# RG-LRU stage: TensorE's order written out, sigmoid work between the gates, PSUM banks of its own; the later adaLN vectors summed in the q/k/v stage

## The chip, the cores and the metric

The kernel runs on one core of a Trainium2 chip. The metric is the device time of one execution in microseconds (us). PE is TensorE, DVE is VectorE, ACT is ScalarE, POOL is GpSimd, and SP is SyncE, which here only issues DMAs. PSUM is the memory in which matmuls leave their results; it has eight banks per partition, each of 512 float32.

## What is computed

One backbone layer over 1024 latent tokens and 256 context tokens of width 1024, all in float32. Reduced to what matters here:

```python
mod = split(silu(c) @ w_ada + b_ada, 6)            # adaLN: shift/scale 1, gate 1, shift/scale 2, gate 2
z   = split(modulate(rmsnorm(x), mod[0], mod[1]) @ w_in, ...)   # rnn in, rnn gate, q, kv, k rope, merge gates
xr  = conv4(z[0])                                   # width-4 depthwise conv over the tokens
for d in (forward, backward):                       # RG-LRU, two directions
    r, i = sigmoid(xr @ wa[d] + ba[d]), sigmoid(xr @ wx[d] + bx[d])     # block diagonal, 8 blocks of 128
    a = exp(-8 * r * softplus(-lam[d]))
    h[d] = scan(a, sqrt(1 - a * a) * i * xr)
rnn = (h[0] + h[1]) * gelu(z[1])
q, k, v = latent attention projections of z[2:5], rms norms, rope
merged = sigmoid(z[5][0]) * (rnn @ w_rnn_out) + sigmoid(z[5][1]) * (attend(q, k, v) @ w_mla_out)
x = x + mod[2] * (merged @ w_o)
x = x + mod[5] * expert_choice_moe(modulate(rmsnorm(x), mod[3], mod[4]))
```

The vectors `mod[2]` to `mod[5]` (the "later" ones) are not needed before the RG-LRU branch is finished.

## The kernel before

Every float32 matmul is done as three matmuls on a high and a low part (`mm3`, lines 97 to 99: high by high, low by high, high by low). `split` (lines 93 and 94) makes the parts: ACT copies the high part (`wh`, `zh`), DVE subtracts it from the source (`wl`, `zl`). Weights come through a ring of four raw buffers called `wr`, which `nextw` keeps two items ahead.

The program runs through stages. In the first the tokens are normed and kept transposed in SBUF (`xh`, `xl`). In the **q/k/v stage** (function `qkv`, about 80 to 268 us) eight latent token tiles of 128 and then two context tiles are worked on one after the other. For a tile PE does three transposes (`tp`), the projection of the next tile (`zq`, 24 matmuls), `kv` (6), `qp` (12), and then as filling a block of 48 matmuls of the rnn gate or of a merge gate (`z1`, shown as `z`). DVE norms and ropes: `zn` is the normed projection, `kf` and `qf` are the keys and queries, and the rope is lines 439 to 444. The reciprocal roots are powers on POOL (line 142, tile `st`, widths 3, 8 and 16). `k_d`, `v_d`, `q_d`, `ge_d`, `s_d` are stores to DRAM. The Tile scheduler orders the instructions of each engine here.

In the **RG-LRU stage** (268 to 591.5 us) eight channel blocks are worked on. `conv_part` projects a block (`z0` for the latent tokens, shown as `z`, and `z0c` for the context), ACT evicts it (line 589) and DVE adds the other three conv taps (line 592). `lru_part` does the four gates: `gz` (6 matmuls) for the latent and `gc` (3) for the context tokens, each followed by sigmoids on ACT (lines 610 and 611). After tanh, exp and sqrt on ACT and the scans on DVE, `rn_d` is stored. `sig_block` is a merge gate: 48 matmuls into `zg`, a sigmoid and a store; `sig_plan` says how many follow each block (1, 1, 1, 2, 1, 1, 2, 3). ACT's order is written out by hand in this stage; PE's is the scheduler's.

The later adaLN vectors are summed here as well: `mod_step` loads 128 rows of `w_ada` (512 KB) and DVE multiplies them by `silu(c)` and adds them to `acc` (line 395); after eight steps two matmuls of ones with `acc` (`mp`, line 401) sum the partitions, ACT copies the row (line 402) into a tile of tag `sg`, and the row is stored to `mod_d`. Four steps are done after each `sig_block`, 32 in all. `MP2` and `N2` are the numbers of steps after each tile of the q/k/v stage and of all those done there: 1 and 0.

All PSUM tiles of both stages and of the next come from two rings: `a` with three tiles of two banks (`kv`, `qp`, `z1`, `z0`, `gz`, `zg`, `mp`, `ro`) and `b` with two of one bank (`tp`, `zq`, `z0c`, `gc`, `mc`, `lb`). After the RG-LRU stage `mc` and `lb` prepare the router, and `ro` (the rnn branch's output projection, with `rh` and `rl` read back from `rn_d`) begins.

Of the kernel before, what the change touches and what calls it, by code (L numbers as in the profile page):

```python
# [27 lines left out]
P = 128  # L28
# [32 lines left out]
def layer_kernel(ctx: ExitStack, tc: tile.TileContext, I, rope_tab, out, dbg=None):  # L61
# [268 lines left out]
    def nextw(shape):  # L330
        n = taken[0]
        assert items[n][1] == shape, (items[n], shape)
        taken[0] = n + LOOK
        fetch()
        taken[0] = n + 1
        return ahead[n]

    LOOK = 2
    NFIRST = 3
    MP2, N2 = 1, 0  # L340
# [45 lines left out]
    def mod_step(j):  # L386
# [9 lines left out]
        if k == KD - 1:  # L396
            row = mpool().tile([1, D], F32, name="g", tag="sg", bufs=1)
            mp = pa("mp")
            for n in range(2):
                sl = slice(n * 512, (n + 1) * 512)  # L400
                nc.tensor.matmul(mp[0:1, sl], ones, acc[:, sl], start=True, stop=True)
            nc.scalar.copy(row, mp[0:1, :])
            nc.sync.dma_start(mod_d[m:m + 1, :], row)
# [162 lines left out]

    p3c = pool("p3")
    p3 = p3c.__enter__()
    if True:
        p4c = None  # L570

        def sig_block(dst, mid=None):
            zz = pa("zg")
            zblock(zz)
            if mid:
                mid()
            if p4c:
                sg = wst.tile([P, SEQ], F32, name="wr", tag="wr", bufs=4)
            else:
                sg = p3.tile([P, SEQ], F32, name="sg", tag="sg", bufs=1)  # L580
            nc.scalar.activation(sg, zz, AF.Sigmoid)
            nc.sync.dma_start(dst, sg)

        def conv_part(b):
            zc, zz = pb("z0c"), pa("z0")
# [12 lines left out]
        def lru_part(b, xr, xrh, xrl):  # L598
            gh, gl_ = nextw([2, 2, P])
            gates = []  # L600
            for d in range(2):
                for g, bn in ((0, "ba"), (1, "bx")):
                    gc, gz = pb("gc"), pa("gz")
# [4 lines left out]
                    r = p3.tile([P, TOK], F32, name=("r", "i")[g], bufs=2)  # L608
# [4 lines left out]
            av, vv = [], []  # L613
            for d in range(2):
                v = p3.tile([P, TOK], F32, name="vv", bufs=2)
                nc.scalar.activation(v, gates[2 * d], AF.Tanh, scale=p8[:, d * 8 + b:d * 8 + b + 1])
                vv.append(v)
            for d in range(2):
# [28 lines left out]
            return rest  # L647
# [13 lines left out]
        with tc.manual_schedule(engines={mybir.EngineType.Activation}):  # L661
# [21 lines left out]
            for b in range(KD):  # L683
# [3 lines left out]
                rest = lru_part(b, *cur)  # L687
                if b + 1 < KD:
                    split(nxt[1], nxt[2], nxt[0])
                for n in range(sig_plan[b]):  # L690
                    w, bb = jobs.pop(0)
                    if b == KD - 1 and n == 1:
                        assert not steps
# [3 lines left out]
                    sig_block((s0_d, s1_d)[w][bb], rest if n == 0 else load_rn if b == KD - 1 else None)  # L697
                    for _ in range(4):
                        if steps:
                            mod_step(steps.pop(0))  # L700
            load_rn(KD)


    xnp.__exit__(None, None, None)
# [504 lines left out]
```

## Time and profile before

| | us |
|---|---|
| median of 3 runs | 1798.1 (1798.03 to 1804.27) |
| the profiled execution, its own time | 1810.5 |
| its span, first to last instruction | 1808.7 |
| mean granted TensorE clock | 0.972 |
| PE busy | 1693.9 (94%) |
| DVE, ACT, POOL busy | 1365.1, 1042.9, 272.9 |

The profile is of one execution, which took 12.4 us longer than the median of the runs; 1.8 us of its own time lie outside the span. A busy share is one of the whole span. An engine that idles costs nothing by itself: what matters is where PE, the busiest one, stands still, and what it waits for there.

### The profile page before, as it was taken

How to read it: one execution, taken by the hardware profiler on the slowest of the kernel's cores; microseconds unless marked ns; L12 is line 12 of the kernel's file. 1: busy time of each engine (PE TensorE's matmuls, PEld its weight loads, DVE VectorE, ACT ScalarE, POOL GpSimd, SP SyncE). 2: the span in 40 equal slices, each digit the busy share in tenths (PEclk: the TensorE clock that was granted, in tenths of full speed). 3: DMA queues.
4: the chain of work that ended last, by engine and by line, in shares of the span. 5: the costliest groups of instructions: out<-in, count | busy, mean ns of one | idle time of the engine just before them, and what ended most of it. 6: DMA issues, size and time to landing. Idle time of an engine off the chain costs nothing.

```text
span 1808.7 us, 21761 instructions
## 1 busy us (share of the span) xinstructions
PE 1693.9 (94%) x7769; PEld 1351.6 (75%) x7769; DVE 1365.1 (75%) x1840; ACT 1042.9 (58%) x1323; POOL 272.9 (15%) x204
## 2 busy tenths in 40 slices
PE   8999999999999999999999989809999999999996
PEld 4888888777778877777776767707888888888875
DVE  5754546997897445787885866587999999999996
ACT  3532325665676314677667443306777777777784
POOL 2033321121211100011110031310010011001000
PEclk8999999999999999999999998959999999999999
DMA  9255343455443943001000566468999999999971
GB/s 345 94 161 120 92 119 94 141 162 163 140 134 113 311 148 130 28 28 47 9 1 1 221 232 235 168 249 286 377 369 393 395 386 368 399 385 378 380 265 24
DMA packets 178380, 365.91 MB, mean 202 GB/s; under 512 B 43328, under 2 KB 93912, under 8 KB 178272
## 3 DMA queue, kind: packets, MB, share of 16 engines
q1 hardware_dynamic: 173664, 347.74, 53.4%
q0 software_dynamic: 4608, 16.78, 4.0%
q8 instruction: 61, 1.00, 0.2%
q14 instruction: 47, 0.39, 0.1%
HBM read 316.94 MB, written 47.54 MB: 202 GB/s over the span
## 4 chain that ended last, share of the span: by engine, by line
PE 67%; DVE 16%; issue 6%; ACT 5%; DMA 3%; POOL 2%; SPq 0%; POOLq 0%; DVEq 0%; ACTq 0%
PE w_e_gate L98 3%; PE w_e_up L98 3%; PE w_e_gate L97 3%; PE w_e_gate L99 3%; PE w_e_down L98 3%; PE w_e_up L99 3%; PE w_e_up L97 3%; PE w_e_down L99 3%; PE w_e_down L97 3%; PE pm L782 2%; POOL st L142 2%; PE s L97 2%; PE ro L97 2%; PE ro L99 2%; PE ro L98 2%
## 5 line engine op out<-in xcount | busy, mean ns | idle before, releaser
L94 DVE TENSOR_TENSOR wl<-ma,wh 128x1024 fp32r<-128x1024 f32 x198 | 236.1, 1220 | 21.5 <-ACT wh L93 14.8
L93 ACT CAST wh<-ma 128x1024 fp32r<-128x1024 f32 x198 | 206.7, 1053 | 57.0 <-PE w_e_down L99 18.1
L94 DVE TENSOR_TENSOR wl<-me,wh 128x1024 fp32r<-128x1024 f32 x142 | 170.0, 1220 | 20.4 <-ACT wh L93 14.4
L93 ACT CAST wh<-wr 128x1024 fp32r<-128x1024 f32 (+1 forms) x97 | 98.3, 1014 | 147.6 <-PE z L98 54.6
L93 ACT CAST wh<-me 128x1024 fp32r<-128x1024 f32 x142 | 148.3, 1053 | 45.7 <-PE w_e_down L99 15.6
L846 ACT ACTIVATE pr<-s 128x512 f32<-128x512 f32 x160 | 95.6, 599 | 75.4 <-PE s L99 74.0
L784 DVE TENSOR_REDUCE mx<-pm 128x1 f32<-128x320 f32 x256 | 114.5, 483 | 24.9 <-PE pm L782 22.6
L94 DVE TENSOR_TENSOR wl<-wr,wh 128x1024 fp32r<-128x1024 f32 (+1 forms) x97 | 114.5, 1188 | 22.5 <-ACT wh L93 20.7
L98 PE MATMUL z<-xl,wh 128*128 128x512 f32 x320 | 126.5, 396 | 0.8 <-DVE xl L279 0.8
L99 PE MATMUL z<-xh,wl 128*128 128x512 f32 x320 | 126.2, 395 | 0.6 <-POOL wl L325 0.6
L97 PE MATMUL z<-xh,wh 128*128 128x512 f32 x320 | 126.4, 397 | 0.0
L1155 POOL DMA_INDIRECT out_dram<-y,icol x16 | 36.3, 2266 | 494.5 <-DVE y L1154 494.5
L94 DVE TENSOR_TENSOR pl<-pr,ph 128x1024 fp32r<-128x1024 f32 x64 | 81.2, 1269 | 31.8 <-ACT ph L93 25.0
L98 PE MATMUL w_e_up<-wl,xgh 128*128 128x512 f32 x256 | 103.1, 403 | 1.0 <-DVE wl L94 0.9
L98 PE MATMUL w_e_gate<-wl,xgh 128*128 128x512 f32 x256 | 102.7, 401 | 0.0
L97 PE MATMUL w_e_gate<-wh,xgh 128*128 128x512 f32 x256 | 102.4, 400 | 0.0
L98 PE MATMUL w_e_down<-wl,hdh 128*128 128x512 f32 x256 | 101.6, 397 | 0.6 <-DVE wl L94 0.2
L99 PE MATMUL w_e_down<-wh,hdl 128*128 128x512 f32 x256 | 99.8, 390 | 0.8 <-DVE hdl L94 0.8
L99 PE MATMUL w_e_gate<-wh,xgl 128*128 128x512 f32 x256 | 100.3, 392 | 0.0
L97 PE MATMUL w_e_down<-wh,hdh 128*128 128x512 f32 x256 | 99.9, 390 | 0.2 <-ACT hdh L93 0.2
L97 PE MATMUL w_e_up<-wh,xgh 128*128 128x512 f32 x256 | 100.1, 391 | 0.0
L99 PE MATMUL w_e_up<-wh,xgl 128*128 128x512 f32 x256 | 100.1, 391 | 0.0
(336 smaller groups left out, 4433.3 us busy)
## 6 DMA issues: line engine op xcount, KB each, us to landing
ma<-in_w_e_down_dram SPq DMA_DIRECT2D x68, 512.0 KB, 8.5
ma<-in_w_e_gate_dram SPq DMA_DIRECT2D x66, 512.0 KB, 7.5
ma<-in_w_e_up_dram SPq DMA_DIRECT2D x64, 512.0 KB, 6.6
me<-in_w_e_gate_dram SPq DMA_DIRECT2D x48, 512.0 KB, 5.6
me<-in_w_e_up_dram SPq DMA_DIRECT2D x48, 512.0 KB, 7.0
me<-in_w_e_down_dram SPq DMA_DIRECT2D x46, 512.0 KB, 8.2
wr<-in_w_in_dram SPq DMA_DIRECT2D x32, 512.0 KB, 4.9
wr<-in_w_ada_dram SPq DMA_DIRECT2D x32, 512.0 KB, 3.5
```

What stands on the lines that cost most here:

```text
L93: nc.scalar.copy(h, src)
L94: nc.vector.tensor_tensor(l, src, h.bitcast(F32), OP.subtract)
L97: nc.tensor.matmul(o, lh, rh, start=start, stop=False)
L98: nc.tensor.matmul(o, lh, rl, start=False, stop=False)
L99: nc.tensor.matmul(o, ll, rh, start=False, stop=stop)
L142: nc.gpsimd.tensor_tensor(ap, ap, h, OP.pow)
L782: nc.tensor.matmul(pm[:, 0:320], qh[:, t * P:(t + 1) * P], kh[:, g * 320:(g + 1) * 320], start=True, stop=True)
L784: nc.vector.tensor_reduce(mx[:, g, t:t + 1], pm[:, 0:320], axis=AX.X, op=OP.max)
L846: nc.scalar.activation(pr[:, sl], sp_, AF.Exp)
L1155: nc.gpsimd.indirect_dma_start(out=out_rows, out_offset=bass.IndirectOffsetOnAxis(ap=icol[:, e:e + 1], axis=0), in_=y, in_offset=None, com ...
```

## The change

1. `MP2, N2 = 4, 4 * KD`: all 32 `mod_step`s are done in the q/k/v stage, four after each of its first eight tiles. Their loads, sums, `mp` matmuls and stores move there. The row is copied into `acc` itself and stored from there.
2. In the RG-LRU stage PE's order is written out too. `sig_mm` is a generator that gives the 48 matmuls of a sigmoid block in eight pieces of six; one piece follows each gate, the other four pieces follow the gates. For that a weight is taken earlier (`look`, `look_ahead`).
3. The stage has its own PSUM pool `ps3`: `z0c` one bank, `gc` one bank, `gz` one buffer of two banks, and `z` (for `z0` and `zg`) a ring of two. After the stage another pool `ps4` has the rings `a` and `b` again.
4. A direction's tanh follows its two gates, and `r` has three buffers.

```diff
@@ -327,17 +327,23 @@
                 split(h, l, raw)
             ahead.append((h, l))
 
-    def nextw(shape):
+    def nextw(shape, look=None):
         n = taken[0]
         assert items[n][1] == shape, (items[n], shape)
-        taken[0] = n + LOOK
+        taken[0] = n + (LOOK if look is None else look)
         fetch()
         taken[0] = n + 1
         return ahead[n]
 
+    def look_ahead():
+        n = taken[0]
+        taken[0] = n - 1 + LOOK
+        fetch()
+        taken[0] = n
+
     LOOK = 2
     NFIRST = 3
-    MP2, N2 = 1, 0
+    MP2, N2 = 4, 4 * KD
 
     def zhalf(dst, h, l, n, ks=range(KD)):
         sl = slice(CTX + n * 512, CTX + (n + 1) * 512)
@@ -394,7 +400,7 @@
         nc.sync.dma_start(raw, w_ada[k * P:(k + 1) * P, (2 + m) * D:(3 + m) * D])
         nc.vector.scalar_tensor_tensor(acc, raw, sc[:, k, 0:1], acc, op0=OP.mult, op1=OP.add)
         if k == KD - 1:
-            row = mpool().tile([1, D], F32, name="g", tag="sg", bufs=1)
+            row = acc[0:1, :]
             mp = pa("mp")
             for n in range(2):
                 sl = slice(n * 512, (n + 1) * 512)
@@ -564,14 +570,31 @@
                     mod_step(steps.pop(0))
 
 
+
+
+    assert not steps
+    open_psum("ps3")
+
+    def pz(name):
+        return ps["p"].tile([P, 1024], F32, name=name, tag="z", bufs=2)
+
     p3c = pool("p3")
     p3 = p3c.__enter__()
     if True:
         p4c = None
 
-        def sig_block(dst, mid=None):
-            zz = pa("zg")
-            zblock(zz)
+        def sig_mm(look=None):
+
+            zz = pz("zg")
+            h, l = nextw([KD, P], look)
+            for n in range(2):
+                for k in range(0, KD, 2):
+                    zhalf(zz, h, l, n, (k, k + 1))
+                    yield zz
+
+        def sig_block(dst, mid=None, mm=None):
+            for zz in mm or sig_mm():
+                pass
             if mid:
                 mid()
             if p4c:
@@ -582,7 +605,7 @@
             nc.sync.dma_start(dst, sg)
 
         def conv_part(b):
-            zc, zz = pb("z0c"), pa("z0")
+            zc, zz = ps["p"].tile([P, 512], F32, name="z0c", bufs=1), pz("z0")
             zblock(zz, zc[:, 0:CTX])
             xr = p3.tile([P, TOK], F32, name="xr", bufs=2)
             for o, src, n in ((0, zc, CTX), (CTX, zz, SEQ)):
@@ -597,24 +620,27 @@
 
         def lru_part(b, xr, xrh, xrl):
             gh, gl_ = nextw([2, 2, P])
-            gates = []
+            gates, vv = [], []
+            zg = sig_mm(1)
             for d in range(2):
                 for g, bn in ((0, "ba"), (1, "bx")):
-                    gc, gz = pb("gc"), pa("gz")
+                    gc = ps["p"].tile([P, 512], F32, name="gc", bufs=1)
+                    gz = ps["p"].tile([P, 1024], F32, name="gz", bufs=1)
                     for n in range(2):
                         sl = slice(CTX + n * 512, CTX + (n + 1) * 512)
                         mm3(gz[:, n * 512:(n + 1) * 512], gh[:, g, d], gl_[:, g, d], xrh[:, sl], xrl[:, sl], True, True)
                     mm3(gc[:, 0:CTX], gh[:, g, d], gl_[:, g, d], xrh[:, 0:CTX], xrl[:, 0:CTX], True, True)
-                    r = p3.tile([P, TOK], F32, name=("r", "i")[g], bufs=2)
+                    next(zg)
+                    r = p3.tile([P, TOK], F32, name=("r", "i")[g], bufs=3 - g)
                     bias = col(bn, d * 8 + b)
                     nc.scalar.activation(r[:, CTX:], gz, AF.Sigmoid, bias=bias)
                     nc.scalar.activation(r[:, 0:CTX], gc[:, 0:CTX], AF.Sigmoid, bias=bias)
                     gates.append(r)
-            av, vv = [], []
-            for d in range(2):
                 v = p3.tile([P, TOK], F32, name="vv", bufs=2)
                 nc.scalar.activation(v, gates[2 * d], AF.Tanh, scale=p8[:, d * 8 + b:d * 8 + b + 1])
                 vv.append(v)
+            look_ahead()
+            av = []
             for d in range(2):
                 r, gi = gates[2 * d:2 * d + 2]
                 a = p3.tile([P, TOK], F32, name="av", bufs=2)
@@ -644,7 +670,7 @@
                 nc.vector.tensor_tensor(ge, ge, hf[:, LT], OP.mult)
                 nc.sync.dma_start(rn_d[b], ge)
 
-            return rest
+            return rest, zg
 
         rh, rl = [], []
 
@@ -658,7 +684,7 @@
 
         jobs = sig_jobs[n_early:]
         cur_pool.append(p3)
-        with tc.manual_schedule(engines={mybir.EngineType.Activation}):
+        with tc.manual_schedule(engines={mybir.EngineType.Activation, mybir.EngineType.PE}):
             nxt = conv_part(0)
 
             sp = consts.tile([P, 8, 16], F32, name="sp")
@@ -684,23 +710,21 @@
                 cur = nxt
                 if b + 1 < KD:
                     nxt = conv_part(b + 1)
-                rest = lru_part(b, *cur)
+                rest, zg = lru_part(b, *cur)
                 if b + 1 < KD:
                     split(nxt[1], nxt[2], nxt[0])
                 for n in range(sig_plan[b]):
                     w, bb = jobs.pop(0)
                     if b == KD - 1 and n == 1:
-                        assert not steps
                         p3c.__exit__(None, None, None)
                         p4c = pool("p4")
                         p4 = p4c.__enter__()
-                    sig_block((s0_d, s1_d)[w][bb], rest if n == 0 else load_rn if b == KD - 1 else None)
-                    for _ in range(4):
-                        if steps:
-                            mod_step(steps.pop(0))
+                    sig_block((s0_d, s1_d)[w][bb], rest if n == 0 else load_rn if b == KD - 1 else None,
+                              zg if n == 0 else None)
             load_rn(KD)
 
 
+    open_psum("ps4")
     xnp.__exit__(None, None, None)
 
     wr = consts.tile([P, KD, NE], F32, name="wrt")
```

TensorE at the first two gates of the second block, before. `gz` and `gc` are a gate's two PSUM tiles.

```order
L97 MATMUL gz_2758<-xrh_2494,wh_2578 128x512
L98 MATMUL gz_2758<-xrl_2495,wh_2578 128x512
L99 MATMUL gz_2758<-xrh_2494,wl_2579 128x512
L97 MATMUL gc_2757<-xrh_2494,wh_2578 128x256
L98 MATMUL gc_2757<-xrl_2495,wh_2578 128x256
L99 MATMUL gc_2757<-xrh_2494,wl_2579 128x256
L97 MATMUL gz_2772<-xrh_2494,wh_2578 128x512
L98 MATMUL gz_2772<-xrl_2495,wh_2578 128x512
L99 MATMUL gz_2772<-xrh_2494,wl_2579 128x512
```

The same place after, with the sigmoid block's tile `zg`.

```order
L97 MATMUL gz_2875<-xrh_2626,wh_2722 128x512
L98 MATMUL gz_2875<-xrl_2627,wh_2722 128x512
L99 MATMUL gz_2875<-xrh_2626,wl_2723 128x512
L97 MATMUL gc_2874<-xrh_2626,wh_2722 128x256
L98 MATMUL gc_2874<-xrl_2627,wh_2722 128x256
L99 MATMUL gc_2874<-xrh_2626,wl_2723 128x256
L97 MATMUL zg_2885<-xh_127,wh_2781 128x512
L98 MATMUL zg_2885<-xl_128,wh_2781 128x512
L99 MATMUL zg_2885<-xh_127,wl_2782 128x512
...
L97 MATMUL gz_2896<-xrh_2626,wh_2722 128x512
L98 MATMUL gz_2896<-xrl_2627,wh_2722 128x512
L99 MATMUL gz_2896<-xrh_2626,wl_2723 128x512
```

A gate was followed by the next gate, and now six matmuls of a sigmoid block stand between two gates.

VectorE in the third tile of the q/k/v stage, before, from the last multiplication of the keys to the queries' gain.

```order
L493 TENSOR_TENSOR kf_1181<-kf_1181,gk_658 128x8x64
L517 TENSOR_REDUCE st_988<-sq_1211 128x8
L518 TENSOR_TENSOR st_988<-st_988,invq_99 128x16
L519 TENSOR_SCALAR st_988<-st_988 128x16
L526 TENSOR_TENSOR qf_1218<-qp_1198,st_988 128x4x64
L528 TENSOR_TENSOR qf_1218<-qp_1198,st_988 128x4x32
...
L530 TENSOR_TENSOR qf_1218<-qf_1218,gq_655 128x8x96
```

The same after; `acc_1325` is the sum of the second of the later vectors, `wr` the loaded rows.

```order
L499 TENSOR_TENSOR kf_1213<-kf_1213,gk_658 128x8x64
L523 TENSOR_REDUCE st_1003<-sq_1243 128x8
L401 SCALAR_TENSOR_TENSOR acc_1325<-wr_1328,sc_122,acc_1325 128x1024
L524 TENSOR_TENSOR st_1003<-st_1003,invq_99 128x16
L401 SCALAR_TENSOR_TENSOR acc_1325<-wr_1331,sc_122,acc_1325 128x1024
L525 TENSOR_SCALAR st_1003<-st_1003 128x16
L401 SCALAR_TENSOR_TENSOR acc_1325<-wr_1334,sc_122,acc_1325 128x1024
L532 TENSOR_TENSOR qf_1250<-qp_1230,st_1003 128x4x64
L534 TENSOR_TENSOR qf_1250<-qp_1230,st_1003 128x4x32
...
L401 SCALAR_TENSOR_TENSOR acc_1325<-wr_1337,sc_122,acc_1325 128x1024
L536 TENSOR_TENSOR qf_1250<-qf_1250,gq_655 128x8x96
```

Two sums stand ahead of line 525, which gives the 16-wide power its input, one stands behind it, and one between the multiplications of `qf`. POOL's queue in this stage with what it waits for, before.

```order
L499 COPY kf<-kr 128x8x32 [waits DVE_49]
L522 MEMSET qf 128x8 [waits DMAHW0_49]
L142 TENSOR_TENSOR st<-st,eps 128x3 [waits DVE_49,Activation_49]
L142 TENSOR_TENSOR st<-st,eps 128x8 [waits DVE_49]
L142 TENSOR_TENSOR st<-st,eps 128x16 [waits DVE_49]
```

The same after, where `acc` is the next vector's sum.

```order
L505 COPY kf<-kr 128x8x32 [waits DVE_49]
L528 MEMSET qf 128x8 [waits DMAHW1_49]
L396 MEMSET acc 128x1024 [waits DMAHW3_49,Activation_49]
L142 TENSOR_TENSOR st<-st,eps 128x3 [waits DVE_49,Activation_49]
L142 TENSOR_TENSOR st<-st,eps 128x8 [waits DVE_49]
L142 TENSOR_TENSOR st<-st,eps 128x16 [waits DVE_49]
```

The memset of the next `acc` has come between the memset of `qf` and the power of `st`; it waits for a DMA.

TensorE at the end of the RG-LRU stage with its waits, before.

```order
L99 MATMUL zg_4553<-xh_127,wl_4413 128x512
L711 MATMUL mc_4653<-ident_88,mrow2_4651 128x16 [waits DMAHW1_49]
L97 MATMUL ro_4708<-rh0_4540,wh_4486 128x512 [waits PE_49,Activation_49]
L98 MATMUL ro_4708<-rl0_4541,wh_4486 128x512 [waits DVE_49]
L99 MATMUL ro_4708<-rh0_4540,wl_4487 128x512
...
L97 MATMUL ro_4708<-rh1_4546,wh_4486 128x512 [waits Activation_49]
...
L717 MATMUL lb_4658<-wrt_4649,mc_4655 128x16 [waits DMAHW3_49,DVE_49]
```

The same after; the tile numbers of `rh` and `rl` are those of the channel blocks.

```order
L99 MATMUL zg_4553<-xh_127,wl_4427 128x512
L735 MATMUL mc_4657<-ident_88,mrow2_4655 128x16 [waits DMAHW1_49]
L97 MATMUL ro_4712<-rh0_4540,wh_4486 128x512 [waits Activation_49]
L741 MATMUL lb_4662<-wrt_4653,mc_4659 128x16 [waits DMAHW3_49,DVE_49]
L98 MATMUL ro_4712<-rl0_4541,wh_4486 128x512
L99 MATMUL ro_4712<-rh0_4540,wl_4487 128x512
```

In both the first `ro` matmul waits for an instruction of ACT. Before it also waits for PE, for the tile that used its buffer last; after, its tile is the first two-bank one of the pool `ps4`. `lb` comes earlier.

## Rows read from the trace of the kernel before

**Rows 1.** The head of the page: the span, busy time with share and instructions.

```profile
span 1808.7 us, 21761 instructions
PE 1693.9 (94%) x7769; PEld 1351.6 (75%) x7769; DVE 1365.1 (75%) x1840; ACT 1042.9 (58%) x1323; POOL 272.9 (15%) x204
```

**Rows 2.** Windows: length; busy us of PE, PEld, DVE, ACT, POOL; clock; DMA share; GB/s.

```profile
80.00:268.00 188.00, 184.03 (x895) 160.61 (x894) 96.93 (x287) 59.36 (x121) 57.12 (x51) 0.99 0.49 126
268.00:591.50 323.50, 309.05 (x1448) 250.26 (x1446) 263.84 (x225) 203.95 (x208) 55.20 (x21) 0.99 0.44 138
```

**Rows 3.** PE's waits, 268 to 592 us (total, times, longest); timeline at 522 us.

```profile
PE gc L97 <- DVE xr L592: 10.6, 7, 3.7
PE gz L97 <- ACT r L610: 3.8, 6, 0.6
...
522.89 0.50 PE L97 MATMUL gz<-xrh,wh 128*128 128x512 f32 x1 [0.64 <-ACT r L610]
```

**Rows 4.** Instructions with the tile mp, and ACT's wait before its copies.

```profile
L401 PE MATMUL mp<-acc,ones 128*1 128x512 f32 x16 | 7.5, 591 | 0.0
...
  DMA s_d<-sg: 18.0, 4
```

**Rows 5.** The window with the slow spell, columns as in rows 2.

```profile
450.00:500.00 50.00, 44.61 (x204) 35.17 (x203) 42.56 (x35) 33.42 (x35) 13.85 (x5) 0.97 0.46 142
```

**Rows 6.** Timeline from one rope's end to the next: start, us, instruction, wait before it.

```profile
193.14 0.28 DVE L444 TENSOR_TENSOR qf<-qf,rtmp 128x128 f32<-128x128 f32 x1
...
199.05 0.11 POOL L522 MEMSET qf<- 128x8 f32 x1 [3.73 <-DMA q_d<-qf]
...
209.15 0.42 DVE L526 TENSOR_TENSOR qf<-qp,st 128x256 f32<-128x256 f32 x1 [3.01 <-POOL st L142]
...
212.67 0.28 DVE L444 TENSOR_TENSOR qf<-qf,rtmp 128x128 f32<-128x128 f32 x1
```

**Rows 7.** Timeline: zl and the kv matmul that needs it, second and seventh tile.

```profile
116.35 0.54 DVE L94 TENSOR_TENSOR zl<-tp,zh 128x384 fp32r<-128x384 f32 x1
...
118.36 0.40 PE L99 MATMUL kv<-ukv,zl 128*128 128x512 f32 x1
...
214.51 0.55 DVE L94 TENSOR_TENSOR zl<-tp,zh 128x384 fp32r<-128x384 f32 x1
...
215.12 0.19 PEld L99 LDWEIGHTS kv<-ukv,zl 128*128 128x128 f32 x1 [0.40 <-DVE zl L94]
```

**Rows 8.** The sums (shortest, median, longest ns), and one beside POOL.

```profile
L395 DVE SCALAR_TENSOR_TENSOR acc<-wr,sc,acc x32: 1254/1280/3987, 282.5 to 529.8; 128x1024 f32<-128x1024 f32 x32
...
375.68 3.98 DVE L395 SCALAR_TENSOR_TENSOR acc<-wr,sc,acc 128x1024 f32<-128x1024 f32 x1
...
374.70 3.88 POOL L624 TENSOR_TENSOR i<-i,xr 128x1280 f32<-128x1280 f32 x1 [1.50 <-ACT i L611]
```

**Rows 9.** The tiles acc and mod_d: POOL's memset (ns), the row's store.

```profile
L390 POOL MEMSET acc<- x4: 952/954/954, 272.1 to 471.3; 128x1024 f32 x4
...
DMA to landing us min/median/max: 6.9/6.9/6.9
```

**Rows 10.** PE's timeline at the last context tile.

```profile
265.41 0.27 PE L474 MATMUL tp<-ident,zn 128*128 128x128 f32 x1
...
267.13 0.50 PE L97 MATMUL kv<-ukv,zh 128*128 128x512 f32 x1
```

**Rows 11.** Timeline at the end of the RG-LRU stage, PE and ACT.

```profile
559.91 2.62 ACT L616 ACTIVATE vv<-r,sp 128x1280 f32<-128x1280 f32 x2
...
590.91 0.39 PE L98 MATMUL zg<-xl,wh 128*128 128x512 f32 x1
591.13 0.39 PE L99 MATMUL zg<-xh,wl 128*128 128x512 f32 x1
...
591.62 0.50 PE L97 MATMUL ro<-rh,wh 128*128 128x512 f32 x1
...
596.28 1.02 ACT L581 ACTIVATE wr<-zg 128x1024 f32<-128x1024 f32 x1
```

## The prediction

> **What bounds the kernel now.** The head of the page comes first: TensorE (PE) is busy 1693.9 of 1808.7 us [rows 1], so a change helps where PE waits, and costs where it makes PE wait. The table by windows then says where the two stages that the change touches lose time [rows 2]: the q/k/v stage (80 to 268 us) keeps PE busy 184.0 of 188.0 us, the RG-LRU stage (268 to 591.5 us) 309.1 of 323.5. The list of PE's waits names those 14.4 us completely [rows 3]: 10.6 us in which the matmuls of `gc` wait for VectorE's (DVE's) conv taps (they hold `z0c`, which shares a ring of two banks with `gc`), and 3.8 us in which `gz` waits for ScalarE's (ACT's) sigmoid of an earlier gate. Four pairs of `mp` matmuls stand there too, 7.5 us in all [rows 4]. After the longest of these waits there is a spell in which the granted clock is at the lower of its two levels (1.2 GHz, not 2.4): the mean is 0.97 in the 50 us around it, some 1.5 us lost [rows 5].
>
> The timeline of the q/k/v stage shows what the page hides. PE is full there, but a second chain runs round with almost the same period: the rope of one token tile ends on DVE (193.42), the store of `q_d` leaves, GpSimd's (POOL's) memset of the next `qf` waits for it to land (199.05), the small power `st` stands behind that memset in POOL's queue, then come DVE's `zn`, two more powers on POOL, and the next rope, which ends at 212.95 [rows 6]: 19.5 us. PE's own period is (215.12 - 118.36) / 5 = 19.4 us [rows 7]. After each rope come `wl` and `zl`, and PE's `kv` needs `zl`. At the second tile `zl` is ready 1.5 us before PE needs it; six tiles on PE waits for it (0.40 us). So this stage has two bounds within one per cent of each other, and whatever lengthens the DVE/POOL chain lengthens the stage.
>
> **The change part by part.** *Gates.* No work is dropped; PE gets six sigmoid matmuls (6 x 0.23 = 1.4 us, the spacing of the `zg` rows in [rows 11]) after each gate, and `z0c`, `gc` and `gz` get banks of their own. The 10.6 us for `z0c` go: `gc` no longer needs its bank. The slow spell goes with the wait before it: 1.5 us. Of the `gz` waits one stays in each of seven blocks, since `gz` is now a single buffer: the second gate waits until the first one's sigmoid has read it, and that sigmoid starts late because ACT first evicts the next block's conv. Before, with the third buffer, the fourth `gz` met the same sigmoid and waited 0.64 us [rows 3]; after, 1.4 us of cover end at about the same moment, so I keep 7 x 0.64 = 4.5 us. Gain 14.4 + 1.5 - 4.5 = 11.4 us; bounds 0 (the single bank costs as much as it frees) and 15.9.
>
> *The vector sums leave the RG-LRU stage.* There PE loses the `mp` pairs: 7.5 us gain. DVE loses 32 sums there, which were not on PE's path except through the taps counted above. ACT's 18.0 us in front of the row copies [rows 4] was idle time of an engine for which PE did not wait then: nothing.
>
> *They arrive in the q/k/v stage.* One undisturbed sum takes 1.28 us, spaced 1.25 us [rows 8]. DVE runs in order, and the new order puts them at given places. Those behind a power's input lie in a wait for POOL (the one at 209.15 is 3.0 us long [rows 6]) and cost nothing if they run there undisturbed; those behind `zl` lie in the wait for `q_d` (3.73 us on POOL [rows 6]) and are free too. The others push the rope: in the tiles 2, 4 and 6 three each (two ahead of the input of the 16-wide power, one between the `qf` multiplications), in the tiles 0 and 1 two each, so 13; and one stands between the last rope and the last `zl`. 14 x 1.25 = 17.5 us, since the slack at the end is nil. Below, all could be hidden (0); above, see the port rival.
>
> *The store of the row.* POOL's memset of the next `acc` reuses the buffer that the row's store reads, and it stands ahead of the power for the next `zn` twice (vectors 1 and 2; for vector 3 it stands behind). That store follows `q_d` and `ge_d` in SP's queue, so it leaves about 1.0 us after the rope's end (an estimate: those two are issued first); it took 6.9 us to land, and the memset 0.95 [rows 9]. `q_d` landed 5.6 us after the rope [rows 6]. So the power is late by 1.0 + 6.9 + 0.95 - 5.6 = 3.2 us, twice: 6.4 us. If the store lands with `q_d`, only 2 x 0.95 = 1.9 remain. I take the measured landing.
>
> *The four `mp` pairs here.* 1.9 us each. Three fall where PE would wait for the lengthened chain anyway, the last one is followed by a context tile that has no such chain: 1.9 us, 7.5 if the chain is not what binds. Stage in all: 17.5 + 6.4 + 1.9 = 25.8 us, between 7.5 and 32.4.
>
> *The seam.* Before, the last `tp` and the last `kv` are 1.7 us apart, and 13 `z0c` matmuls of the next stage fill that [rows 10]. With a pool of its own and a fixed order the RG-LRU stage starts after `kv`, so PE waits for `zh`: 1.5 us.
>
> *The tail.* Before, the first `ro` matmul starts 0.5 us after the last `zg` one, in a third buffer [rows 11]. After, its tile lies in the new pool, on banks that the last two `zg` blocks hold, so it waits for the sigmoid that reads the last one. That sigmoid is queued on ACT behind copies of `rh` which wait for loads behind the last `rn_d` store, and ended at 597.3, 5.8 us after PE's last `zg`. It also comes later against PE: behind the last gate PE now has 126 sigmoid matmuls and not 144, 18 x 0.23 = 4.1 us less, of which an earlier tanh (2.62 us for two) gives 1.3 back. 5.8 + 2.8 = 8.6 us of wait, less some 0.9 us which PE idled there already: 7.7 us. Bounds 0 and 10.
>
> **Sum:** -11.4 - 7.5 + 25.8 + 1.5 + 7.7 = **+16.1 us**. The profiled execution took 1810.5 us, 12.4 above the median of the runs; on its own time that makes 1826.6, on the median 1798.1 + 16.1 = **1814 us**, slower by 0.9%.
>
> **A rule against the change.** One sum that started while POOL ran `L624` took 3.98 us instead of 1.28 and ended 1.1 us after POOL's instruction [rows 8]. So a sum placed in a wait for a power may not be hidden: six of them stand there, and each would end about 1.1 us after the power: 6.6 us more. The Trainium skill ("GPSIMD Engine Reference", Specifications) says that GpSimd shares its SBUF interfaces with VectorE and contends with instructions that read two SBUF operands. The row agrees with it; no run here shows a sum beside one of these small powers.
>
> **The rivals.**
> 1. *The chain has room* (other side, faster). DVE is idle 91 of 188 us in the q/k/v stage [rows 2], and 32 sums need 40. If the waits in the chain close up around them, 17.5 + 6.4 us go and the stage costs 1.9: 16.1 - 23.9 = -7.8, 1790 us. Against it: the order puts 13 of them where DVE is not waiting. It decides the sign once 16 of those 24 us are hidden.
> 2. *The sums do not hide behind powers*: +6.6, 1821 us.
> 3. *The tail does not wait*, because the sigmoid comes earlier than the loads let it now: 16.1 - 7.7 = +8.4, 1806.5 us. For it: SP has less to carry there; against it: the same order of copies and loads on ACT and SP.
> 4. *The gates do not gain* (the change doesn't do what it says): one `gz` bank makes PE wait for each sigmoid in place of `z0c`: +27.5, 1825.6 us. Against it: 1.4 us of cover.
>
> **How the numbers follow.** Forecast 0.38, rival 1 0.20, rival 2 0.17, rival 3 0.13, rival 4 0.12. A measurement tells about 0.5% (9 us) from no change. Slower by more (over 1807): the forecast, 2, 4 and part of 3, 0.66. Within: most of 3 and half of 1, 0.21. Faster: the rest of 1, 0.13. The range takes in rivals 1 to 4 at their values: 1790 to 1825 us; the forecast's own is 1807 to 1821.
>
> **What would show it.** In the profile after: PE's waits at `gc` for the taps are gone and some 0.6 us per block stays at `gz`; no `mp` in the RG-LRU stage, which is some 19 us shorter; in the q/k/v stage the distance of two ropes rises to 22 to 24 us in the tiles 2, 4 and 6, with PE waiting at `kv` for `zl` there, and the `acc` memset releasing a late `st`; at the stage's end one wait of 6 to 9 us at the first `ro`, released by a sigmoid. The prediction is wrong if PE's period in the q/k/v stage stays near 19.4 us, if the gates still wait, or if the first `ro` starts at once.

## The result and the profile after

The changed kernel takes 1827.1 us (median of 4 runs, 1820.05 to 1829.61) against 1799.2 us of the kernel before on the same chip: ratio 1.014, 95% interval [1.0109, 1.0172]. It is slower, as forecast, but by 25 us (that ratio; 28 by the two medians) and not by 16; the time lies 2 us above the range. Its profiled execution, 1820.05 us, is the shortest of its runs.

The stages are cut in one way for every kernel here: q/k/v from the first `tp` matmul to the last `kv` one, RG-LRU from there to the last `zg`, `ro` from there to the last `ro` matmul, and the rest of the program behind.

| us, in the profiled execution | q/k/v | RG-LRU | ro | rest | its time |
|---|---|---|---|---|---|
| before | 176.0 | 322.7 | 101.9 | 1115.7 | 1810.5 |
| after | 203.4 | 304.8 | 110.5 | 1107.8 | 1820.05 |
| difference | +27.4 | -17.9 | +8.6 | -7.9 | +9.6 |

The three stages that the change touches are 18.1 us longer. The rest, the same work in both, is 7.9 us shorter here; it varies from execution to execution (below). The stage in front of the four columns isn't listed.

The head of the page of after, to be held against [rows 1]:

```profile
span 1818.3 us, 21770 instructions
PE 1692.5 (93%) x7769; PEld 1352.1 (74%) x7769; DVE 1368.7 (75%) x1840; ACT 1043.1 (57%) x1323; POOL 278.3 (15%) x204
```

Nothing is to be seen there: the busy times are those of before. The windows of after by stage (columns as in [rows 2]) show it:

```profile
92.00:295.00 203.00, 184.79 (x845) 153.77 (x844) 128.72 (x310) 55.55 (x113) 65.20 (x53) 0.96 0.69 184
295.00:600.00 305.00, 299.05 (x1443) 250.08 (x1441) 231.66 (x193) 200.00 (x204) 49.47 (x17) 1.00 0.28 89
600.00:711.00 111.00, 102.65 (x463) 83.51 (x462) 46.23 (x72) 22.09 (x26) 5.07 (x8) 0.94 0.59 202
```

In the q/k/v stage PE now idles 203.0 - 184.8 = 18.2 us; over the 176.0 us of before the same view gives:

```profile
92.40:268.40 176.00, 173.07 (x843) 151.19 (x844) 91.52 (x279) 52.45 (x110) 56.26 (x50) 0.99 0.47 119
```

That was 2.9 us of idling. So 15.3 us of the growth are waits. PE's busy time grew by 11.7 us: 7.5 for the `mp` matmuls, less 1.5 for 13 `z0c` matmuls that stand in the next stage now, which leaves 5.7. That remainder I put down to the lower granted clock (mean 0.96 for 0.99), at which the same matmuls take longer. The first list of PE's waits is that of the q/k/v stage (92 to 290 us), the second that of the RG-LRU stage (322 to 600 us), columns as in [rows 3].

```profile
PE kv L99 <- DVE zl L94: 15.2, 5, 4.4
```

```profile
PE gz L97 <- ACT r L636: 5.8, 7, 2.0
```

The wait of `kv` for `zl` is the one foretold. The seam shows as well, in the list from 100 to 720 us; its longer wait ends at 293.84 us, at the last `kv`:

```profile
PE kv L97 <- ACT zh L93: 2.0, 2, 1.4
```

The timeline of the third tile shows how the wait for `zl` comes about; it answers to [rows 6, 7].

```profile
138.09 0.28 DVE L450 TENSOR_TENSOR qf<-qf,rtmp 128x128 f32<-128x128 f32 x1
...
144.64 0.16 DVE L465 TENSOR_TENSOR st<-st,invn 128x3 f32<-128x3 f32 x1 [4.14 <-ACT sq L463]
144.84 0.17 DVE L466 TENSOR_SCALAR st<-st 128x3 f32<-128x3 f32 x1
...
152.36 1.28 DVE L401 SCALAR_TENSOR_TENSOR acc<-wr,sc,acc 128x1024 f32<-128x1024 f32 x1
...
153.68 1.28 DVE L401 SCALAR_TENSOR_TENSOR acc<-wr,sc,acc 128x1024 f32<-128x1024 f32 x1
154.88 0.17 DVE L525 TENSOR_SCALAR st<-st 128x16 f32<-128x16 f32 x1
155.00 1.28 DVE L401 SCALAR_TENSOR_TENSOR acc<-wr,sc,acc 128x1024 f32<-128x1024 f32 x1
159.07 0.42 DVE L532 TENSOR_TENSOR qf<-qp,st 128x256 f32<-128x256 f32 x1 [2.79 <-POOL st L142]
...
160.14 1.27 DVE L401 SCALAR_TENSOR_TENSOR acc<-wr,sc,acc 128x1024 f32<-128x1024 f32 x1
...
163.66 0.28 DVE L450 TENSOR_TENSOR qf<-qf,rtmp 128x128 f32<-128x128 f32 x1
163.86 1.28 DVE L401 SCALAR_TENSOR_TENSOR acc<-wr,sc,acc 128x1024 f32<-128x1024 f32 x1
...
166.36 0.55 DVE L94 TENSOR_TENSOR zl<-tp,zh 128x384 fp32r<-128x384 f32 x1
```

POOL over the same stretch and in the two tiles behind it, then PE:

```profile
144.40 0.11 POOL L528 MEMSET qf<- 128x8 f32 x1 [4.10 <-DMA q_d<-qf]
144.95 0.96 POOL L396 MEMSET acc<- 128x1024 f32 x1 [0.43 <-DMA mod_d<-acc]
145.86 0.85 POOL L142 TENSOR_TENSOR st<-st,eps 128x3 f32<-128x3 f32 x1
...
155.12 3.91 POOL L142 TENSOR_TENSOR st<-st,eps 128x16 f32<-128x16 f32 x1 [4.92 <-DVE st L525]
...
177.43 2.90 POOL L142 TENSOR_TENSOR st<-st,eps 128x16 f32<-128x16 f32 x1 [2.74 <-DVE st L525]
...
190.87 0.96 POOL L396 MEMSET acc<- 128x1024 f32 x1 [0.67 <-ACT sq L463]
192.00 0.85 POOL L142 TENSOR_TENSOR st<-st,eps 128x3 f32<-128x3 f32 x1 [0.17 <-DVE st L466]
```

```profile
166.96 0.80 PE L99 MATMUL kv<-ukv,zl 128*128 128x512 f32 x1 [3.94 <-DVE zl L94]
167.56 0.63 PE L97 MATMUL kv<-ukv,zh 128*128 128x512 f32 x1
167.99 0.63 PE L98 MATMUL kv<-ukv,zh 128*128 128x512 f32 x1
```

From the rope's end at 138.37 to the next at 163.94 it is 25.6 us, where [rows 6] had 19.5. The 6.1 us have three parts. Three sums stand ahead of the rope (152.36, 153.68 and 160.14), 3.3 us over the spacing of the same instructions in the tile of [rows 6]. The 16-wide power is 1.0 us longer than in the next tile, where no sum stands beside it (3.91 for 2.90). And the first power `st` starts 7.5 us behind the rope and not 5.7: it stands behind the memset of `acc`, which waits for the row's store and ends at 145.91. Of these 1.8 us the memset costs about 0.9, since the other input of `st`, line 466, ends only at 145.01 (DVE had waited for `sq`, and so for PE's `zq`). The other such memset costs nothing: at 192.00 `st` waits for line 466 alone. One more sum stands between the rope and `zl`. Then PE waits 3.94 us, and its next matmuls are spaced 0.43 and not 0.23 us: the lower clock.

At the end of the RG-LRU stage, PE and ACT, to be held against [rows 11]:

```profile
608.79 0.79 PE L97 MATMUL ro<-rh,wh 128*128 128x512 f32 x1 [8.35 <-ACT wr L604]
```

```profile
607.72 1.02 ACT L604 ACTIVATE wr<-zg 128x1024 f32<-128x1024 f32 x1
```

PE waits 8.35 us at the first `ro` matmul for the last block's sigmoid.

### The profile page after: what moved, and what is told of

It reads as the page before. It is cut to its first block, busy times and chain, and to the rows that moved or that the text cites. A ratio compares the mean times of both kernels' runs of the same rounds, so it can differ in the third digit from the quotient of the medians.

```text
span 1818.3 us, 21770 instructions
## 1 busy us (share of the span) xinstructions
PE 1692.5 (93%) x7769; PEld 1352.1 (74%) x7769; DVE 1368.7 (75%) x1840; ACT 1043.1 (57%) x1323; POOL 278.3 (15%) x204
## 4 chain that ended last, share of the span: by engine, by line
PE 73%; DVE 11%; ACT 6%; issue 4%; DMA 3%; POOL 2%; SPq 0%; POOLq 0%; ACTq 0%; DVEq 0%
PE w_e_gate L98 3%; PE w_e_up L98 3%; PE w_e_gate L97 3%; PE w_e_gate L99 3%; PE w_e_down L98 3%; PE w_e_up L99 3%; PE w_e_up L97 3%; PE w_e_down L99 3%; PE w_e_down L97 3%; PE z L98 3%; PE z L99 3%; PE z L97 3%; PE pm L806 2%; PE s L97 2%; PE ro L97 2%
## 5 line engine op out<-in xcount | busy, mean ns | idle before, releaser
L94 DVE TENSOR_TENSOR wl<-wr,wh 128x1024 fp32r<-128x1024 f32 (+1 forms) x97 | 129.0, 1337 | 54.2 <-ACT wh L93 52.5
L99 PE MATMUL w_e_down<-wh,hdl 128*128 128x512 f32 x256 | 99.8, 390 | 0.8 <-DVE hdl L94 0.8
```

The lines of the kernel that those rows point to most:

```text
L94: nc.vector.tensor_tensor(l, src, h.bitcast(F32), OP.subtract)
L99: nc.tensor.matmul(o, ll, rh, start=False, stop=stop)
```

## The experiments

The theory was that the sums are dear in the q/k/v stage, that the written order and the own banks gain at the gates, and that the tail pays for the banks. Its main rival for the gates: they gained only because the sums had left. Rivals for the q/k/v stage: the loads of `w_ada` bind, not the sums, or the place of the sums does. The first four kernels ran on one chip (before 1805.1 us), the next four on another (1805.3 us) and the last four on a third (1805.4 us).

| us, in the profiled execution | q/k/v | RG-LRU | ro | rest | median | ratio, 95% |
|---|---|---|---|---|---|---|
| e0, before again | 176.6 | 323.7 | 99.8 | 1110.0 | 1806.5 | 1.0011 [0.9995, 1.0026] |
| e1, vectors only | 205.8 | 303.8 | 103.4 | 1109.4 | 1818.6 | 1.0081 [1.0053, 1.0109] |
| e2, order only | 178.5 | 335.9 | 110.4 | 1108.1 | 1829.6 | 1.0149 [1.0119, 1.0180] |
| e3, other banks for `ro` | 208.9 | 313.9 | 110.5 | 1111.7 | 1833.2 | 1.0161 [1.0131, 1.0191] |
| e4, few sums | 201.8 | 306.6 | 110.8 | 1115.0 | 1823.1 | 1.0096 [1.0081, 1.0112] |
| e5, after again | 205.5 | 306.4 | 110.4 | 1108.6 | 1829.7 | 1.0142 [1.0126, 1.0157] |
| e6, sums after `zl` | 213.8 | 316.1 | 103.4 | 1109.7 | 1838.1 | 1.0181 [1.0166, 1.0196] |
| e7, tail plan | 205.4 | 306.6 | 107.2 | 1108.0 | 1822.9 | 1.0105 [1.0089, 1.0122] |
| e8, vectors in attention | 176.7 | 304.2 | 100.8 | 1135.3 | 1811.0 | 1.0031 [1.0014, 1.0048] |
| e9, e8 with the order | 179.1 | 304.8 | 106.4 | 1133.3 | 1820.5 | 1.0101 [1.0082, 1.0120] |
| e10, no loads | 202.6 | 306.4 | 110.8 | 1114.4 | 1826.8 | 1.0122 [1.0104, 1.0141] |
| e11, few sums, no loads | 189.4 | 306.4 | 110.6 | 1114.2 | 1811.7 | 1.0048 [1.0025, 1.0072] |

**e0 and e5: both kernels again, no edit.**

> The kernel before, unchanged, once more, for a second profile: the three stages up to the end of ro were 17 us longer in the profile after, but the runs differ by 25 us, and the profile before was 12 us above its runs. If the profiled execution of before was simply a long one in the later stages: about 1800 us with the same first 693 us and 8 to 10 us less behind them. If before's executions differ in the stages that the change touches: the difference shows up there.

> The changed kernel once more, for a second profile: the profiled execution after was the shortest of its runs by 5 us. If the executions differ in the q/k/v stage (in the kernels with the sums there it took 203 to 209 us from the first tp to the last kv, with a mean granted clock of 0.93 to 0.96), this one shows a longer q/k/v stage with a lower clock, about 208 us, and a time of 1825 to 1829. If they differ behind ro: the same 203 us and more in the later stages.

The stages repeat within 3 us; the rest of the program, which no edit but that of e8 and e9 touches, took 1107.8 to 1115.7 us.

**e1: the kernel before with the vectors alone.**

```diff
-    MP2, N2 = 1, 0
+    MP2, N2 = 4, 4 * KD
...
-            row = mpool().tile([1, D], F32, name="g", tag="sg", bufs=1)
+            row = acc[0:1, :]
```

> The kernel before with the first part of the change alone: all 32 vector sums in the q/k/v stage, the row kept in the sum's tile; the RG-LRU stage and its banks as before. If the sums and memsets on the chain of ropes are what costs: the q/k/v stage 24 to 27 us longer, the RG-LRU stage 7 to 9 us shorter (four mp pairs gone), no wait at the first ro, in all +16 to +20 us (about 1816). If the sums fit into DVE's idle time and the q/k/v stage is long for another reason: -5 us or less (about 1794).

PE's waits in its RG-LRU stage (326 to 604 us):

```profile
PE gc L97 <- ACT r L611: 4.0, 4, 1.0
PE gc L97 <- DVE xr L592: 1.8, 3, 0.9
PE gz L97 <- ACT r L610: 1.0, 1, 1.0
```

The old order in the old banks loses 18.9 us in this stage when the sums go, as much as the changed kernel (17.9, with 1.5 us of `z0c` more in the stage); I had expected 7 to 9. All of PE's waits there come to 6.8 us, and to 5.8 in the changed kernel. The waits for the conv taps fall from 10.6 us [rows 3] to 1.8: the taps had been late because sums stood ahead of them in DVE's queue. The kernel before shows it at 525.73 us, where `gc` waits 0.84 us for a tap:

```profile
519.63 1.28 DVE L395 SCALAR_TENSOR_TENSOR acc<-wr,sc,acc 128x1024 f32<-128x1024 f32 x1
...
522.41 1.28 DVE L395 SCALAR_TENSOR_TENSOR acc<-wr,sc,acc 128x1024 f32<-128x1024 f32 x1
...
525.20 0.47 DVE L592 SCALAR_TENSOR_TENSOR xr<-z0c,colv,xr 128x255 f32<-128x255 f32 x1
```

**e2: the order alone**, the changed kernel with the sums behind each sigmoid block of the RG-LRU stage again (four each; the `mp` pair one block later, in the bank of `gz`; `r` with two buffers).

```diff
-    MP2, N2 = 4, 4 * KD
+    MP2, N2 = 1, 0
...
+            mp = ps["p"].tile([P, 1024], F32, name="gz", bufs=1)
...
+                    mod_row()
+                    for _ in range(4):
+                        if steps:
+                            mod_step(steps.pop(0))
```

> The changed kernel with the vector sums back in the RG-LRU stage (r in two buffers as before, the mp pair one sigmoid block later and in gz's banks): the written order, the pieces between the gates and the own banks alone. If the terms of the prediction hold: gates -11, seam +1.5, tail +8, in all -2 us (about 1797), with the wait of 8 us at the first ro. If the tail and the seam are no cost: -11 us (about 1788). If the single gz bank eats what the gates gain: +8 us or more.

PE's waits in that stage (270 to 610 us):

```profile
PE zg L99 <- DVE wl L94: 7.5, 2, 3.8
PE gz L97 <- ACT r L643: 7.4, 5, 2.2
PE gz L97 <- ACT g L416: 7.4, 1, 7.4
```

The stage grew by 13 us instead of shrinking. But 14.9 us of its waits (for `wl`, which stands behind sums in DVE's queue, and for a row copy that stands in front of a sigmoid) come from where I put sums and copies, so this run doesn't settle what the order is worth. e9 does, for a stage without the sums; what it would be worth beside them stays open.

**e3: other banks for the first `ro` tile**, three unused tiles at the head of `ps3`.

```diff
+    for nm, w in (("gc", 512), ("z0c", 512), ("gz", 1024)):
+        ps["p"].tile([P, w], F32, name=nm, bufs=1)
```

> The changed kernel with the pool of the RG-LRU stage laid out in another order of banks, so that the first ro tile lies where gz lay and waits for no sigmoid. If that sigmoid is the cause of the tail: 7 to 8 us less than the changed kernel. If it is only the first of a row of waits (PE's order takes the first ro tile whole, and its last operand rh7 was ready at 617.8 us, 18 us after the last zg matmul): 0 to 1 us less, with waits for rh4 to rh7 in place of the one wait.

The first `ro` starts at once (616.4, the last `zg` 615.9), and the `ro` stretch is as long as in the changed kernel (110.5 us). In PE's timeline another wait has come:

```profile
625.15 3.60 PE L744 MATMUL lb<-wrt,mc 128*128 128x16 f32 x16 [8.24 <-DVE mc L740]
```

So the bank was only the first in a row of waits. (The whole is no faster either: in the new layout the first `z0` matmul waits 4.8 us for ACT's eviction of `vf`, and the RG-LRU stage is 7.5 us longer than in e5.)

**e7: more cover at the tail**, one sigmoid block moved from the fourth channel block to the last.

```diff
-    sig_plan = [1, 1, 1, 2, 1, 1, 2, 3]
+    sig_plan = [1, 1, 1, 1, 1, 1, 2, 4]
```

> The changed kernel with one sigmoid block moved from the fourth channel block behind the last one (four there, not three). If the tail is the lateness of the last block's chain (its rh7 comes 18 us after PE's last zg matmul): 10.9 us more cover, the wait at the first ro falls from 8.4 to about 1 us and the stretch from the last zg to the last ro from 110 to about 103; 7 us less than the changed kernel. If the wait comes from the order of ACT's queue (the sigmoid of the last zg is behind the copies in any case): the wait stays above 5 us.

```profile
609.40 0.80 PE L97 MATMUL ro<-rh,wh 128*128 128x512 f32 x1 [5.31 <-ACT wr L604]
```

In that timeline the wait has fallen from 8.35 to 5.31 us with 11 us more of matmuls in front of it (48 at 0.23 us), the stretch from 110.5 to 107.2. I had expected about 1 us; a wait above 5 was the sign of the rival, that the order of ACT's queue holds the sigmoid. The median is 6.9 us below that of e5, more than the stretch explains.

**e4: 24 of the 32 sums cut to 32 columns** (the other columns of these sums are left out).

```diff
-        nc.vector.scalar_tensor_tensor(acc, raw, sc[:, k, 0:1], acc, op0=OP.mult, op1=OP.add)
+        w = D if k in (0, KD - 1) else 32
+        nc.vector.scalar_tensor_tensor(acc[:, 0:w], raw[:, 0:w], sc[:, k, 0:1], acc[:, 0:w], op0=OP.mult, op1=OP.add)
```

> The changed kernel with six of each vector's eight sums cut to 32 of 1024 columns (0.15 us and not 1.28; the later vectors are then wrong), every instruction in its place. If the sums on the chain of ropes set the q/k/v stage: nine sums and the four delays of 16-wide powers fall away, 12 to 15 us less in that stage (203 becomes about 190) and with it in the whole. If the stage is long through the loads, the stores or the mp pairs: 3 us less at most.

The stage is only 1.6 us shorter than in after, 3.7 than in e5, where I had expected 12 to 15. The waits of DVE and of PE in it (92 to 290 us) say why:

```profile
DVE acc L402 <- DMA wr<-in_w_ada_dram: 22.0, 8, 5.3
```

```profile
PE kv L97 <- ACT zh L93: 9.1, 3, 5.2
PE kv L99 <- DVE zl L94: 2.6, 2, 1.6
```

Where the sums were, DVE now waits for their loads; in after that wait was 2.5 us. PE waits 2.6 us for `zl` instead of 15.2, but 9.1 for `zh`, whose copy stands in ACT's queue behind that of a weight which is loaded late.

**e10: the sums without the loads** (they read a slice of `xh` in place of the rows of `w_ada`), **and e11: both**, e10 with the sums of e4.

```diff
-        raw = wst.tile([P, D], F32, name="wr", tag="wr", bufs=4)
-        nc.sync.dma_start(raw, w_ada[k * P:(k + 1) * P, (2 + m) * D:(3 + m) * D])
+        raw = xh[:, k, 0:D].bitcast(F32)
```

> The kernel after, its sums reading a slice of x that lies in SBUF already instead of a loaded tile of w_ada: the 32 loads are gone, the 32 sums stay, the later vectors are wrong. Theory (the ring of raw tiles and the SP queue are a second limit about as tight as the sums): q/k/v stage falls from 203 to 206 us only to 195 to 202, as when the sums were cut, ACT's wait for wr in that stage falls from 33 us to under 15, kv still waits for DVE. Rival A (the loads are the limit): the stage falls below 190. Rival B (the sums alone are): stays at 203 or more.

> As the kernel without loads, and 24 of the 32 sums cut to 32 columns. Theory (two limits, either one enough): the q/k/v stage falls to 184 to 190, that is 176 and the four matmul pairs with a little of the memsets. Rival (the rest, matmul pairs, memsets and powers, holds it): stays above 197.

PE's first wait in the stage, in e10 and then in e11:

```profile
PE kv L99 <- DVE zl L94: 14.0, 4, 5.1
```

```profile
PE kv L99 <- DVE zl L94: 6.0, 3, 2.8
```

Without the loads the stage stays at 202.6 us: my expectation of 195 to 202 was missed, and while the full sums are there the loads cost nothing. With both gone it falls to 189.4. So there are two limits, either enough to hold the stage above 200 us, and taking one away shows almost nothing. The 13.4 us that e11 still has over before hold the four `mp` pairs (7.5 us of PE), eight whole sums, the memsets and the seam; no run takes them apart.

**e6: the sums behind `zl`**, where the working of the prediction has a free gap; DVE's order written out, on the kernel before.

```diff
+    counts = [4, 4, 0, 4, 4, 0, 4, 4, 0, 8]
...
+            for _ in range(counts.pop(0)):
+                mod_step(steps.pop(0))
...
+        with tc.manual_schedule(engines={mybir.EngineType.DVE}):
```

> The kernel before with the vector sums in the q/k/v stage, but in DVE's order written out: four after zl, where DVE waits for q_d to land, in the tiles 0, 1, 3, 4, 6 and 7, and eight in the last context tile; the RG-LRU stage as before without its sums. If the place of the sums is what costs and their departure is what frees the gates: q/k/v stage 8 to 13 us longer than before (185 to 190), RG-LRU stage 17 to 19 us shorter, in all 5 to 11 us faster than before (about 1797). If any sum in the q/k/v stage costs its time: 25 us or more there, slower than before by 8 us or more.

```profile
PE kv L99 <- DVE zl L94: 24.0, 7, 5.8
```

PE's wait for `zl` became longer, and the last `mp` pair waits 7.6 us more for its sums, at 319.61 us in the RG-LRU stage. This place is no better; since all of DVE's order changed with it, the run says no more than that.

**e8 and e9: the sums in the attention stage**, behind `ro`, on the kernel before (e8) and on the changed one (e9). Each row is added in two sums of 512 columns, and the router's preparation moves behind attention.

```diff
...
+                if i % 2 == 0 and steps:
+                    mod_step(steps.pop(0))
+                if i % 16 == 1 and 1 < i < 66:
+                    mod_row(i // 16 - 1)
...
```

> The kernel before with its own PE order and PSUM layout; the sums of the four later vectors move out of the RG-LRU stage into the attention stage (one weight row of 128 every second step, as two sums of 512 columns each, the pair of matmuls per vector two steps later), and the router's preparation that reads them moves behind the attention stage. Theory (the sums' departure alone frees the RG-LRU stage, and their price is set by where they go): RG-LRU stage 322.7 to about 304 us as in the run with the vectors only; q/k/v stage stays at 176; the attention stage, where VectorE is busy 237.8 of 318 us and the DMA engines 0.09, grows by the matmul pairs, 7.6 us, and little else: in all 10 us less than before, ratio about 0.994. Rival A (DVE's place in the attention stage is as tight as in the q/k/v stage, because PE waits there for its row maxima and its subtractions): the stage grows by 20 us or more and the whole is no faster than before. Rival B (the written PE order made the RG-LRU gain): the RG-LRU stage stays at 320 us or more.

> The kernel after (written PE order, own PSUM layout) with the same move of the sums into the attention stage. Theory (the order adds nothing once the sums have gone, and costs the tail): q/k/v stage 177, RG-LRU stage about 305, first ro wait and ro stretch as after, 110 us, so 7 to 9 us longer than the kernel before with the sums in the attention stage. Rival (the order gains, hidden so far by the later start of the stage): RG-LRU stage under 298 us, the whole no longer than that kernel.

The attention stage of before (693.2 to 997.3 us, 304.1) and of e8 (324.3), by windows:

```profile
693.20:997.30 304.10, 292.97 (x1335) 221.28 (x1334) 225.62 (x401) 209.95 (x334) 37.71 (x42) 0.99 0.09 30
```

```profile
675.80:1000.10 324.30, 303.40 (x1352) 222.85 (x1350) 265.52 (x466) 215.34 (x344) 39.78 (x46) 0.99 0.25 79
```

PE's waits in e8 (690 to 1040 us), the first, which the stage of before does not have:

```profile
PE mr L781 <- DVE mx L778: 9.5, 7, 2.2
```

The RG-LRU stage gives the same 18.5 us, and attention takes 20.2: 16 `mp` matmuls of 0.59 us (9.5 us) and 9.5 us in which PE waits for row maxima. By DVE's timeline these stand behind a sum in its queue at five of the six longer waits, and behind other work at the longest (2.2 us). Rival A held, and e8 is 0.3% slower than before. A version with the transposes `mr` issued later might win these 9.5 us back; it wasn't tried.

e9 against e8 is the written order with its banks, sums out of the way. In the RG-LRU stage it is worth nothing that shows (304.8 against 304.2, 1.5 us of it the moved `z0c`), q/k/v is 2.4 us longer, `ro` 5.6. In e9 the `ro` tiles wait, by PE's timeline, for the read-back of the last blocks:

```profile
585.05 0.69 PE L97 MATMUL ro<-rh,wh 128*128 128x512 f32 x1 [4.44 <-ACT rh L93]
```

In e8, where the scheduler's order mixes the first `ro` tiles, the same wait is 2.08 us, and the stretch takes 100.8 us.

## Why the prediction was right, and where it was wrong

**The q/k/v stage with the seam:** 25.8 + 1.5 = 27.3 us predicted, 27.4 measured (e5 against e0: 28.9), and the wait is the one named, `kv` for `zl`. The seam came as it was worked out (1.4 us of waiting for `zh`), and the ropes of the tiles 2, 4 and 6 are 25.6, 25.9 and 24.2 us behind those before them, for a forecast of 22 to 24. That the sum fits so closely is luck, since its parts were off. The two memsets, 6.4 us in the sum, cost about 0.9 us and nothing: the row's store landed 0.43 us behind `q_d` and not 2.3, and the other input of `st` was late as well. In their place came two things that had no term: 1.0 us by which a sum lengthens a power, at five powers, and the 5.7 us that I put down to the lower clock behind the waits. Rival 2 named the first as 1.1 us on DVE's side at six powers; it is POOL's instruction that grows, while no sum took over 1.42 us, so DVE's next work waits all the same. Nor did I see the second limit, the loads; it added nothing, but would have taken most of the gain from any cheaper sum.

**The gates,** the step that failed in its reason: "the 10.6 us for `z0c` go: `gc` no longer needs its bank". They went, the stage lost 17.9 us where 18.9 had been predicted, and the waits left at `gz` are 5.8 us for 4.5. The number came out by luck, not by its reason: e1 gets all of it with the old banks and order, and e9 gets nothing more from the new ones. The taps were late behind the sums, which I had put down as "not on PE's path except through the taps counted above" and then credited to the bank. Rival 4, the gates do not gain, was right that the order gains nothing, but not in its reason (a wait for each sigmoid) and not in its time.

**The tail:** 7.7 us predicted, 8.6 measured, with a first wait of 8.35 us for 8.6. The agreement is in part luck: PE had idled 2.0 us in this stretch before and not 0.9, so the waits grew by 6.3 us, and the other 2.3 are busy time of the same matmuls, which I put down to the lower clock (0.94 in the windows of after, 0.98 before) and which had no term. That the bank causes it is half true: e3 frees the bank and wins nothing, e7 gives cover and wins 3.3. With the router's matmuls out of the way (e9 against e8) 5.6 us remain, and there the wait is for `rh`: in the order of after the first `ro` tile is taken whole and needs all eight.

**Rival 1,** that the chain has room, failed; so did the two other places that I tried. The 32 sums with their matmul pairs cost 18.5 to 18.9 us in the RG-LRU stage, 27 to 30 in the q/k/v stage (after and e1), 20.2 in attention.

**The size.** The three stages give +18.1 us for a sum of +16.1, and +22.2 in the second pair of profiles (e5 against e0). The median moved by 24.5 to 28 us. The profiled executions of after were the shortest of their runs (1820.05 and 1824.25 us, against medians of 1827.1 and 1829.7), so what the usual execution loses beyond these stages isn't in a trace that I have. The longer executions of after also have the lower mean clock (0.967 to 0.969 for 0.970), but where they lose it stays open. One slip in the chances: the forecast and the rivals 2 and 4 alone make 0.67, so "slower by more" with a part of rival 3 should have been above the 0.66 stated.

By the medians the two halves of the change add up: the vectors alone 1.0081, the order on top of them 1.0142, and on top of e8's vectors 1.0101 for 1.0031: each is a loss, of 0.8% and of 0.6 to 0.7%.

## What to carry to other kernels

When a wait names an engine that works in order, ask what stands ahead of the awaited instruction in its queue before crediting the wait to a buffer. Here the sums' departure alone (e1) freed the gates, and with the sums gone the order and the banks added nothing (e9). Before moving work into "idle" time of an engine, look for the chain that the engine is part of: DVE idles 91 of 188 us in the q/k/v stage [rows 2] and yet the move of 40 us of sums made it 27 us longer. And where taking away one suspect changes nothing, take away two together: without the sums the stage is 1.6 us shorter, without the loads 0.8, without both 14.0 (against e5: 3.7, 2.9 and 16.1).

## What the hardware showed

A sum of 1024 columns on DVE that starts just ahead of a 16-wide power on POOL makes the power 3.91 us long instead of 2.90, and is itself not slowed (1.28 us). So it is at four of the eight 16-wide powers of the stage: a sum starts 0.1 to 0.2 us ahead, and they take 3.87 to 3.95 us; the four others, with no sum beside them, take 2.90. One 8-wide power with a sum just ahead takes 2.60 and not 1.64. In [rows 8] a sum beside a long POOL instruction was the one that waited (3.98 us). The Trainium skill ("GPSIMD Engine Reference", Specifications) says that the two engines contend for shared SBUF interfaces; both rows agree with it. In these rows the one that starts second pays, and in the trace of before it goes by the start as well: beside `L624` four sums that started behind it took 3.63 to 3.99 us, and two that started ahead of it 1.27 and 1.28. It doesn't hold for every pair: beside POOL's copies of `kf` neither grew by more than 0.14 us, and an 8-wide power that started together with a sum (173.04 us) took its usual 1.64.

After a wait of 3.94 us PE ran on at the lower of its two granted levels (0.50 from 166.6 to 170.0 us). Such a spell stands at each of the four waits of `kv` for `zl` of 2.7 to 4.4 us, and the mean of the stage is 0.96 for 0.99. By the busy times above that cost about 5.7 us (an estimate: the remainder there) beyond the waits' own 15.2.
